# High-part products first for weight tiles whose low part is added by a transfer, and such low parts for one step of the down projection

## The chip, the cores and the metric

The kernel runs on one core of a Trainium2 chip. Its time is the device time of one execution, in microseconds; several executions give a median. The profile shows one execution of the same program with the start and end of every instruction. Engines are named as in the profile: PE (matrix products), PEld (loading of the stationary operand), ACT, DVE, POOL, and SP, which only issues transfers here; POOL issues transfers too.

## The reference

One decoder layer over 512 tokens of width 1024, in float32:

```python
u = rmsnorm(h, norm1_g)
proj = u @ w_in            # conv GLU | q | k | v | gate r | low-rank decay | merge gates
c = a_glu[..., :1024] * sigmoid(a_glu[..., 1024:])
c = silu(layernorm(causal_dwconv(c, width=31)));  y_conv = c @ w_conv_out
o = gla_chunked(q, k, v, decay);  y_gla = (rms(o) * silu(r)) @ w_gla_out
h = h + (sigmoid(gate_a) * y_conv + sigmoid(gate_b) * y_gla) @ w_o
z = causal_dwconv(rmsnorm(h, norm2_g) @ w_ffn_up, width=3)
h = h + (silu(z[..., :2816]) * z[..., 2816:]) @ w_ffn_down
return rmsnorm(h, final_g)
```

Every large product is made to nearly float32 precision from float32r parts: each operand is split into a high part and a low part (`x = hi + lo`), and three products are summed: low·high, high·low, high·high.

## The kernel before

**Tiles of weights.** All weights pass through one list, `order`, as tiles of 128 partitions by 1024 float32 (512 KB). `load()` issues the transfer of a tile into one of four `raw` buffers from SP. `split_weight()` makes the two parts in one of four `whi` and one of four `wlo` buffers: ACT copies `raw` to `hi`, which rounds it, and the low part is made in one of two ways. For most tiles DVE subtracts, `lo = raw - hi` (lines 324 and 351). For the tiles named in `ADDED` (part of `w_glu`, all of `w_qk`, `w_gb`, `w_gla`, part of `w_up`) ACT writes `lo = -raw` rounded in the same way (line 344), and POOL issues a transfer that reads the weight from DRAM a second time and adds it to `lo` (line 345). `weight()` hands a tile to the products and asks `prefetch(2)` to emit the splits of the next two tiles.

**Products.** `mm3` emits the three products of one block of 128 rows, lines 395, 396 and 397, in the order low·high, high·low, high·high of its two arguments. `col_tile` calls it eight times with the weights as the stationary operand: 24 products of 512 columns. The first needs `wlo`. This is used for `w_glu`, `w_qk`, the gates and the up projection.

**The down projection** (`seven`, also used for `w_o`) is a seven-product scheme over halves. Its 22 row tiles come in three groups of pairs (4, 3 and 4 pairs), each run after the up projection of the same rows. The steps of a group are listed in `STEPS`: `a11` for both halves d = 0 and 1 of its pairs, then `a12` d = 0, `s1` d = 0, `a12` d = 1, `s1` d = 1, and then `n2`, `s4`, `n3`, `a22`. Here the activations are the stationary operand and the weights move. Steps `a12` and `n3` use tiles as they are loaded; `a11`, `s1`, `n2` and `a22` work on tiles `kept` over several steps, into which sums are added by DVE (line 277) or by adding transfers from POOL (line 303, after the split of an earlier step). For `n3` a second block is added to the loaded one by a transfer from POOL (line 270, `add_n3`), which is issued when the load is.

**What sets the order.** Outside the stretches marked with `manual_schedule` (the start and the very end of the program), a framework orders each engine's instructions by its own estimate of times, and places the waits. Each engine then works through its own list in that order. A tile's buffer is handed on when its last reader is done.

**Other names below.** Line 813 is a tap of the causal convolution of width 31 on DVE, of which 240 are spread between other work. Line 1150 applies the gate to a head's output on DVE after a power taken on POOL (line 443), and line 1156 transposes that on PE. In the down projection the result of step `a12` is summed in PSUM tiles named `ax`, the others in tiles named `mm`; the activations of step `a12` are `ah` and `al`.

Of the kernel before, what the change touches and what calls it, by code (L numbers as in the profile page):

```python
# [10 lines left out]
F32 = mybir.dt.float32  # L11
# [3 lines left out]
AF = mybir.ActivationFunctionType  # L15
ALU = mybir.AluOpType

P = 128
D = 1024
T = 512  # L20
NT = T // P
KT = D // P
# [23 lines left out]
UP_SEVEN = (6, 7, 10, 11, 14, 15, 18)  # L46
UP_BESIDE = (1, 3, 4, 5, 9, 20, 13, 16, 17)
ADDED |= {("w_up", j) for i in UP_BESIDE for j in (i, FT + i)}
SEVEN = {"w_o": KT // 2, "w_down": FT // 2, "w_r": KT // 2, "w_v": KT // 2}


# [27 lines left out]
def trunk_layer(ctx: ExitStack, tc: tile.TileContext, a: dict, out: bass.AP):  # L79
    nc = tc.nc  # L80
# [88 lines left out]
    late = GLU_AT[0] + GLU_AT[1]  # L169
# [135 lines left out]
    def split_weight(between=None):  # L305
        if len(ready) < len(order):
            while len(raws) <= len(ready):
                load()
            raw = raws[len(ready)]
            name, spec = order[len(ready)]  # L310
            if name in SEVEN or name == "w_up7":
                raw = operand(name, raw, *spec) if name in SEVEN else up_operand(raw, *spec)
                n = raw.shape[-1]
                if name == "w_up7" and spec[1] == "m":
                    both = wp.tile([P, D], F32R, tag="raw", name=nm("wm"), bufs=4)
                    nc.scalar.copy(both[:, :T], raw)
                    nc.vector.tensor_tensor(both[:, T:], raw, both[:, :T].bitcast(F32), ALU.subtract)
                    ready.append((both[:, :T], both[:, T:]))
                    load()
                    return  # L320
                hi = wp.tile([P, D], F32R, tag="whi", name=nm("whi"), bufs=4)[:, :n]
                lo = wp.tile([P, D], F32R, tag="wlo", name=nm("wlo"), bufs=4)[:, :n]
                nc.scalar.copy(hi, raw)  # L323
                pace[0] = nc.vector.tensor_tensor(lo, raw, hi.bitcast(F32), ALU.subtract)  # L324
                if name in SEVEN:
                    sum_on(name, *spec)
                skipped = name in INNER and raws[len(ready)] is None
                ready.append((hi, lo))
                if not skipped:
                    load()  # L330
                return
            hi = wp.tile([P, D], F32R, tag="whi", name=nm("whi"), bufs=4)
            if order[len(ready)][0] == "w_low":
                nc.scalar.copy(hi, raw)
                if order[len(ready)][1] == 0:
                    part_lo = lambda t: t.rearrange("p (k c) -> p k c", c=P)[:, :, :RANK]
                    nc.vector.tensor_tensor(part_lo(hi), part_lo(raw), part_lo(hi.bitcast(F32)), ALU.subtract)
                ready.append((hi, None))
                load()
                return  # L340
            lo = wp.tile([P, D], F32R, tag="wlo", name=nm("wlo"), bufs=4)
            nc.scalar.copy(hi, raw)  # L342
            if order[len(ready)] in ADDED:
                pace[0] = nc.scalar.activation(lo, raw, AF.Copy, scale=-1.0)  # L344
                nc.gpsimd.dma_start(lo, a[name][spec], accum_op=ALU.add)  # L345
                ready.append((hi, lo))
                load()
                return
            if between:
                between()  # L350
            pace[0] = nc.vector.tensor_tensor(lo, raw, hi.bitcast(F32), ALU.subtract)  # L351
            ready.append((hi, lo))
            load()
# [37 lines left out]
    def mm3(acc, l, r, first, last, more=False):  # L391
# [4 lines left out]
        nc.tensor.matmul(acc, lh, rl, start=False, stop=False, **kw)  # L396
        nc.tensor.matmul(acc, lh, rh, start=False, stop=last, **kw)  # L397

    def col_tile(w, acts, acc=None, lo=0, hi=T):

        if acc is None:
            acc = mm_bank()
        for k in range(KT):
            s = slice(k * P, (k + 1) * P)
            ah, al = acts[k]
            mm3(acc[:, lo:hi], (w[0][:, s], w[1][:, s]), (ah[:, lo:hi], al[:, lo:hi]), k == 0, k == KT - 1)
        return acc

    def row_half(name, j0, n, acts, nk, done, tok_inner, middle=None):
# [856 lines left out]
    def seven(name, pairs, acts, complete, at=lambda step, i: None, fine=False):  # L1266
# [19 lines left out]
        def products(step, i, parts, lo=0, hi=T, own=None):  # L1286
            acc = bank[of[step]][i][:, lo:hi] if own is None else own[:, lo:hi]
            opens = step in ("a11", "s1", "a12") or own is not None
            for d, w in parts:
                for j, pair in enumerate(acts[2 * d : 2 * d + 2]):  # L1290
                    ah, al = (x[:, i * P : (i + 1) * P] for x in pair[step])
                    c = slice(j * T + lo, j * T + hi)

                    read = 2 * d + j == len(acts) - 1
                    mm3(acc, (ah, al), (w[0][:, c], w[1][:, c]), opens and d == 0 and j == 0, read, not opens)

        def add_to(t, n, c, x, op=ALU.add):
            nc.vector.tensor_tensor(hres[t, n][:, c], hres[t, n][:, c], x[:, c], op)  # L1298
# [287 lines left out]
    def by_parts(w):  # L1586

        acc = mm_bank()
        for k in range(KT):
            s = slice(k * P, (k + 1) * P)  # L1590
            mm3(acc, (w[0][:, s], w[1][:, s]), acts2[k], k == 0, k == KT - 1)
            yield acc

    for gi, pairs in enumerate(GROUPS):
        acts = []
# [123 lines left out]
```

## Time and profile before

| | us |
|---|---|
| median of 3 runs | 829.84 |
| lowest, highest | 829.54, 833.35 |
| the profiled execution | 828.47 |
| its span, first to last instruction | 826.8 |

The profiled execution took 828.47 us, of which 826.8 us are its span; about 1.7 us lie around it. A row of the timeline has the start in microseconds from the beginning of the span, the duration, engine and line, operation, what is written and what is read, and in brackets how long the engine sat idle before it and what ended that. A list of waits has engine and line, what it waited for, and then total microseconds, times, and the longest.

### The profile page before, as it was taken

The page shows a single profiled execution, that of the slowest core. Times are in us where ns is not written, and L with a number is a line of the kernel's source. Part 1 is how long each engine was busy: PE and PEld are TensorE (multiplying, and loading weights), DVE is VectorE, ACT ScalarE, POOL GpSimd, SP SyncE. Part 2 cuts the span into 40 slices and gives each one's busy share as a digit, 9 for nine tenths or more (in the row PEclk, how much of TensorE's full clock was granted, in tenths as well). Part 3 has the DMA queues.
Part 4 walks back from the last instruction along what each step waited for, and adds up shares of the span by engine and source line. Part 5 has one row for each costly group of instructions (what it writes and reads, how often), then busy time and mean ns, then how long its engine had stood idle before and what let it go on. Part 6 is the DMA issues. An engine that isn't in the chain of part 4 may idle for free.

```text
span 826.8 us, 11023 instructions
## 1 busy us (share of the span) xinstructions
PE 813.3 (98%) x4090; PEld 689.9 (83%) x4090; DVE 676.8 (82%) x991; ACT 471.0 (57%) x669; POOL 123.1 (15%) x144
## 2 busy tenths in 40 slices
PE   8999999999999999999999999999999999999996
PEld 7988878878888888888888898888788888988885
DVE  6898978999989889854689768789858888588896
ACT  7664546695443553359344659655446543667554
POOL 2021101311122121000001012111112111220111
PEclk9999999999999999999999999999999999999999
DMA  9999849558666578221447539356835647557562
GB/s 324 310 327 222 209 116 230 129 160 211 150 131 154 134 195 202 77 102 51 153 92 205 183 116 237 93 146 153 217 93 149 166 89 217 153 153 202 131 128 101
DMA packets 50213, 136.65 MB, mean 165 GB/s; under 512 B 4624, under 2 KB 17184, under 8 KB 50160
## 3 DMA queue, kind: packets, MB, share of 16 engines
q1 hardware_dynamic: 37456, 90.91, 31.2%
q0 software_dynamic: 12528, 44.83, 30.5%
q8 instruction: 32, 0.52, 0.3%
q10 hardware_dynamic: 176, 0.20, 0.1%
q14 instruction: 21, 0.17, 0.1%
HBM read 133.84 MB, written 6.29 MB: 169 GB/s over the span
## 4 chain that ended last, share of the span: by engine, by line
PE 78%; DVE 11%; DMA 4%; issue 3%; ACT 2%; POOL 1%; SPq 0%; POOLq 0%; ACTq 0%; DVEq 0%
PE mm L396 22%; PE mm L395 22%; PE mm L397 22%; DVE c L813 4%; PE ax L395 2%; DMA wlo<-in_w_glu_dram 2%; PE mm L663 2%; PE ax L396 2%; PE ax L397 2%; DVE wlo L324 1%; DMA kept<-rows 1%; DMA x<-in_x_dram 1%; PE ax L1137 1%; DVE tmp L1378 1%; PE ax L474 0%
## 5 line engine op out<-in xcount | busy, mean ns | idle before, releaser
L395 PE MATMUL mm<-uh,wlo 128*128 128x512 f32 (+1 forms) x636 | 237.5, 374 | 3.5 <-DMA wlo<-in_w_glu_dram 1.9
L396 PE MATMUL mm<-ul,whi 128*128 128x512 f32 (+1 forms) x636 | 234.9, 369 | 0.2 <-DVE ul L486 0.2
L397 PE MATMUL mm<-uh,whi 128*128 128x512 f32 (+1 forms) x636 | 234.5, 369 | 0.0
L813 DVE SCALAR_TENSOR_TENSOR c<-h,pp,c 128x507 f32<-128x507 f32 (+20 forms) x240 | 169.9, 733 | 2.8
L395 PEld LDWEIGHTS mm<-uh,wlo 128*128 128x128 f32 x636 | 119.9, 189 | 22.9 <-DMA wlo<-in_w_glu_dram 2.1
L397 PEld LDWEIGHTS mm<-uh,whi 128*128 128x128 f32 x636 | 119.8, 188 | 20.5
L396 PEld LDWEIGHTS mm<-ul,whi 128*128 128x128 f32 x636 | 120.1, 189 | 18.7 <-DVE ul L486 0.7
L342 ACT CAST whi<-raw 128x1024 fp32r<-128x1024 f32 x94 | 97.4, 1042 | 36.7 <-PE mm L397 29.0
L344 ACT ACTIVATE wlo<-raw 128x1024 fp32r<-128x1024 f32 x47 | 49.5, 1058 | 69.6 <-PE mm L395 65.5
L323 ACT CAST whi<-raw 128x1024 fp32r<-128x1024 f32 (+1 forms) x53 | 54.0, 1027 | 52.6 <-PE mm L397 36.1
L324 DVE TENSOR_TENSOR wlo<-raw,whi 128x1024 fp32r<-128x1024 f32 (+1 forms) x53 | 65.8, 1249 | 11.5 <-ACT whi L323 11.0
L1378 DVE SCALAR_TENSOR_TENSOR tmp<-mm,pp,tmp 128x511 f32<-128x511 f32 (+1 forms) x88 | 64.5, 742 | 12.6 <-ACT tmp L1376 12.2
L351 DVE TENSOR_TENSOR wlo<-raw,whi 128x1024 fp32r<-128x1024 f32 x47 | 56.9, 1220 | 16.7 <-ACT whi L342 16.3
L323 ACT CAST whi<-kept 128x1024 fp32r<-128x1024 f32 (+1 forms) x44 | 44.3, 1009 | 37.7 <-PE mm L397 25.6
L324 DVE TENSOR_TENSOR wlo<-kept,whi 128x1024 fp32r<-128x1024 f32 (+1 forms) x44 | 52.3, 1196 | 4.3 <-ACT whi L323 4.1
L1376 ACT ACTIVATE tmp<-mm,pp 128x512 f32<-128x512 f32 x44 | 33.3, 775 | 11.6 <-PE mm L397 11.6
L1298 DVE TENSOR_TENSOR hres<-hres,mm 128x512 f32<-128x512 f32 (+1 forms) x49 | 32.4, 670 | 2.5 <-PE mm L397 2.3
L345 POOL DMA_DIRECT2D wlo<-in_w_up_dram x18 | 15.6, 866 | 95.5 <-ACT wlo L344 77.6
L396 PE MATMUL mm<-wlo,sh 128*128 128x512 f32 x66 | 25.9, 393 | 0.0
L397 PE MATMUL mm<-whi,sh 128*128 128x512 f32 x66 | 25.7, 390 | 0.0
L395 PE MATMUL mm<-h,wlo 128*128 128x512 f32 x64 | 25.4, 397 | 0.0
L395 PE MATMUL mm<-whi,sl 128*128 128x512 f32 x66 | 25.2, 391 | 0.2 <-ACT whi L323 0.2
(361 smaller groups left out, 1635.1 us busy)
## 6 DMA issues: line engine op xcount, KB each, us to landing
raw<-in_w_up_dram SPq DMA_DIRECT2D x44, 512.0 KB, 4.4
wlo<-in_w_up_dram POOLq DMA_DIRECT2D x18, 512.0 KB, 7.4
raw<-in_w_glu_dram SPq DMA_DIRECT2D x16, 512.0 KB, 5.9
raw<-in_w_down_dram SPq DMA_DIRECT2D x15, 512.0 KB, 5.1
kept<-in_w_down_dram POOLq DMA_DIRECT2D x10, 512.0 KB, 5.3
raw<-in_w_v_dram SPq DMA_DIRECT2D x8, 512.0 KB, 6.0
rows<-in_w_r_dram SPq DMA_DIRECT2D x16, 256.0 KB, 6.4
raw<-in_w_qk_dram SPq DMA_DIRECT2D x8, 512.0 KB, 5.1
```

Of the source, the lines that this page charges most:

```text
L323: nc.scalar.copy(hi, raw)
L324: pace[0] = nc.vector.tensor_tensor(lo, raw, hi.bitcast(F32), ALU.subtract)
L342: nc.scalar.copy(hi, raw)
L344: pace[0] = nc.scalar.activation(lo, raw, AF.Copy, scale=-1.0)
L351: pace[0] = nc.vector.tensor_tensor(lo, raw, hi.bitcast(F32), ALU.subtract)
L395: nc.tensor.matmul(acc, ll, rh, start=first, stop=False, **kw)
L396: nc.tensor.matmul(acc, lh, rl, start=False, stop=False, **kw)
L397: nc.tensor.matmul(acc, lh, rh, start=False, stop=last, **kw)
L813: nc.vector.scalar_tensor_tensor(y[:, s:], c[:, : T - s], w, y[:, s:], ALU.mult, ALU.add)
L1298: nc.vector.tensor_tensor(hres[t, n][:, c], hres[t, n][:, c], x[:, c], op)
L1376: nc.scalar.activation(z, acc, AF.Identity, bias=pp[:, PP_FB + m : PP_FB + m + 1], scale=w[2])
L1378: nc.vector.scalar_tensor_tensor(z[:, s:], acc[:, : T - s], w[j], z[:, s:], ALU.mult, ALU.add)
```

## The change

It has three parts.

1. `col_tile` and `by_parts` now take their products from a new generator, `col_products`. For the tiles in a new set, `LOW_LAST_IN` (`w_glu` 4 and 8 and all eight of `w_qk`, all of them tiles whose low part is added), it emits the 16 products with `whi` first and the 8 with `wlo` behind them. For all other tiles the order is as before.
2. In the down projection the tiles of step `a12` (two per group, six in all, one of them half as wide) get their low part as the `ADDED` tiles do: ACT writes `-raw`, and POOL issues a transfer that adds the weight. The subtraction on DVE is gone for them.
3. In `products` of `seven`, the products of step `a12` are sorted so that within one half d the four with `whi` come before the two with `wlo` (two before one where a half has one pair). This holds for `w_o` too, whose low parts are still made by DVE.

```diff
+LOW_LAST_IN = {("w_glu", 4), ("w_glu", 8)} | {("w_qk", m) for m in range(KT)}
...
                 nc.scalar.copy(hi, raw)
-                pace[0] = nc.vector.tensor_tensor(lo, raw, hi.bitcast(F32), ALU.subtract)
+                if name == "w_down" and spec[1] == "a12":
+                    pace[0] = nc.scalar.activation(lo, raw, AF.Copy, scale=-1.0)
+                    src = block(name, spec[0], spec[2], *LOADS[spec[1]])
+                    nc.gpsimd.dma_start(lo, src, accum_op=ALU.add)
+                else:
+                    pace[0] = nc.vector.tensor_tensor(lo, raw, hi.bitcast(F32), ALU.subtract)
...
-                ready.append((hi, lo))
+                ready.append((hi, lo, (name, spec) in LOW_LAST_IN))
...
+    def col_products(w, acts, acc, lo=0, hi=T):
+        late = [(1, 0, k) for k in range(KT)] if w[2:] and w[2] else []
+        todo = [p for k in range(KT) for p in ([(0, 0, k), (0, 1, k)] if late else [(1, 0, k), (0, 1, k), (0, 0, k)])]
+        todo += late
+        for n, (low_w, low_a, k) in enumerate(todo):
+            l, r = w[low_w][:, k * P : (k + 1) * P], acts[k][low_a][:, lo:hi]
+            nc.tensor.matmul(acc[:, lo:hi], l, r, start=n == 0, stop=n == len(todo) - 1)
+            yield n
...
+            todo = []
             for d, w in parts:
                 for j, pair in enumerate(acts[2 * d : 2 * d + 2]):
...
+                    a = [x[:, i * P : (i + 1) * P] for x in pair[step]]
+                    b = [x[:, j * T + lo : j * T + hi] for x in w]
+                    todo += [(n, d, a[low_a], b[low_w]) for n, (low_a, low_w) in enumerate(((1, 0), (0, 1), (0, 0)))]
+                if step == "a12":
+                    todo.sort(key=lambda p: (p[1], p[0] == 1))
+            end = parts[-1][0] == (len(acts) - 1) // 2
+            kw = {} if opens else {"skip_group_check": True}
+            for n, (_, d, l, r) in enumerate(todo):
+                nc.tensor.matmul(acc, l, r, start=opens and d == 0 and n == 0, stop=end and n == len(todo) - 1, **kw)
```

How this moves instructions is shown for three places. A row has the line, the operation, what is written, what is read, and the shape; the lines of the changed kernel are later by the lines added.

The first is PE at the tile `w_glu` 8 (`whi_1068`, `wlo_1069`; `uh` and `ul` are the activations). Before, its start:

```order
L397 MATMUL mm_981<-whi_1032,f_814 128x512
L395 MATMUL mm_1121<-uh_105,wlo_1069 128x512
L396 MATMUL mm_1121<-ul_106,whi_1068 128x512
L397 MATMUL mm_1121<-uh_105,whi_1068 128x512
L395 MATMUL mm_1121<-uh_105,wlo_1069 128x512
```

With the change, its start and its end:

```order
L403 MATMUL mm_981<-whi_1032,f_814 128x512
L412 MATMUL mm_1121<-uh_105,whi_1068 128x512
L412 MATMUL mm_1121<-ul_106,whi_1068 128x512
...
L412 MATMUL mm_1121<-ul_108,whi_1068 128x512
L412 MATMUL mm_1121<-uh_105,wlo_1069 128x512 x4
L412 MATMUL mm_1121<-uh_107,wlo_1069 128x512 x4
L401 MATMUL mm_979<-whi_1075,ul_108 128x512
```

The low part was read by the first product of the tile and is now read by the last eight, behind sixteen others.

The second is POOL's list of transfers in the first group of the down projection (`kept` are sums for `s1` and `a22`, `raw` are the second blocks of `n3`, `wlo_5069` and `wlo_5149` the low parts of `a12` d = 0 and 1). Before:

```order
L303 DMA kept_4851<-in_w_down_dram 128x1024
L303 DMA kept_4874<-in_w_down_dram 128x1024
L270 DMA raw_5185<-in_w_down_dram 128x1024
L270 DMA raw_5208<-in_w_down_dram 128x1024
L303 DMA kept_4851<-in_w_down_dram 128x1024
```

With the change:

```order
L304 DMA kept_4851<-in_w_down_dram 128x1024
L304 DMA kept_4874<-in_w_down_dram 128x1024
L328 DMA wlo_5069<-in_w_down_dram 128x1024
L271 DMA raw_5187<-in_w_down_dram 128x1024
L328 DMA wlo_5149<-in_w_down_dram 128x1024
L271 DMA raw_5210<-in_w_down_dram 128x1024
L304 DMA kept_4851<-in_w_down_dram 128x1024
```

Two transfers are added, and the second stands behind one that adds to the tile of `n3` d = 0. In the other two groups the order is the same.

The third is ACT at the same place (`tmp` is the convolution of the up projection's last tiles). Before:

```order
L323 COPY whi_5068<-raw_4932 128x1024
L1376 ACTIVATE tmp_5058<-mm_4949,pp 128x512
L323 COPY whi_5086<-kept_4851 128x1024
L1376 ACTIVATE tmp_5093<-mm_4924,pp 128x512
L1376 ACTIVATE tmp_5098<-mm_4925,pp 128x512
L323 COPY whi_5147<-raw_4990 128x1024
```

With the change:

```order
L326 ACTIVATE wlo_5069<-raw_4932 128x1024
L324 COPY whi_5068<-raw_4932 128x1024
L1394 ACTIVATE tmp_5058<-mm_4949,pp 128x512
L324 COPY whi_5087<-kept_4851 128x1024
L1394 ACTIVATE tmp_5094<-mm_4924,pp 128x512
L1394 ACTIVATE tmp_5099<-mm_4925,pp 128x512
L326 ACTIVATE wlo_5149<-raw_4990 128x1024
L1409 COPY yh_5064<-w_5052 128x512
L324 COPY whi_5148<-raw_4990 128x1024
```

ACT writes the negative of each `a12` tile ahead of its high part, and one instruction of another kind comes between them for d = 1.

More of the change, by code (lines that the diff above doesn't have):

```diff
@@ L402, in col_tile @@
             acc = mm_bank()
[L403 to L406, printed above, removed]
+        for _ in col_products(w, acts, acc, lo, hi):
+            pass
         return acc
@@ L1288, in products @@
             opens = step in ("a11", "s1", "a12") or own is not None
+            todo = []
             for d, w in parts:
                 for j, pair in enumerate(acts[2 * d : 2 * d + 2]):
[L1291 to L1295, printed above, removed]
+                    a = [x[:, i * P : (i + 1) * P] for x in pair[step]]
[7 more added lines that the diff above has]
+                nc.tensor.matmul(acc, l, r, start=opens and d == 0 and n == 0, stop=end and n == len(todo) - 1, **kw)
         def add_to(t, n, c, x, op=ALU.add):
@@ L1588, in by_parts @@
         acc = mm_bank()
[L1589 to L1592, printed above, removed]
+        for n in col_products(w, acts2, acc):
+            if n % 3 == 2:
+                yield acc
     for gi, pairs in enumerate(GROUPS):
```

## The prediction

> **What bounds the kernel now.** First the page: which engine is full, and at what clock.
>
> ```profile
> span 826.8 us, 11023 instructions
> PE 813.3 (98%) x4090; PEld 689.9 (83%) x4090; DVE 676.8 (82%) x991; ACT 471.0 (57%) x669; POOL 123.1 (15%) x144
> PEclk9999999999999999999999999999999999999999
> ```
>
> PE is busy for 98% of the span, and the granted clock is full in every slice. A change that leaves the number of products alone, as this one does, can only take PE's waits away or add some. So the second view is the list of what PE waited for.
>
> ```profile
> PE mm L395 <- DMA wlo<-in_w_glu_dram: 1.9, 2, 1.7
> PE mm L395 <- DMA wlo<-in_w_qk_dram: 1.6, 1, 1.6
> PE ax L1156 <- DVE o L1150: 0.2, 1, 0.2
> PE mm L395 <- ACT whi L323: 0.2, 1, 0.2
> ```
>
> Waits for an added low part come to 3.5 us, all in `w_glu` and `w_qk`, none in the down projection, where DVE makes the low parts. That is all there is to win, with 0.2 us where `whi` is late. The timeline places them.
>
> ```profile
> 60.90 0.47 PE L395 MATMUL mm<-uh,wlo 128*128 128x512 f32 x1 [0.19 <-DMA wlo<-in_w_glu_dram]
> 106.38 0.50 PE L395 MATMUL mm<-uh,wlo 128*128 128x512 f32 x1 [1.69 <-DMA wlo<-in_w_glu_dram]
> 106.72 0.39 PE L396 MATMUL mm<-ul,whi 128*128 128x512 f32 x1
> 183.56 0.50 PE L395 MATMUL mm<-uh,wlo 128*128 128x512 f32 x1 [1.60 <-DMA wlo<-in_w_qk_dram]
> ```
>
> **Part 1, high products first in `w_glu` and `w_qk`.** Undisturbed, one product starts 0.227 us after the last (the rows at 569.12 and 569.34 below). Sixteen products ahead of the first low one give 16 x 0.227 = 3.6 us of cover, more than the longest of these waits, 1.7 us. So the waits at 60.90 and 106.38 go: 0.19 + 1.69, and the product after a wait also runs 0.1 us longer (0.50 against 0.39), twice: 2.1 us. Is that kept? Behind them comes a stretch in which DVE is full:
>
> ```profile
> 127.57 1.22 DVE L324 TENSOR_TENSOR wlo<-raw,whi 128x1024 fp32r<-128x1024 f32 x1 [1.74 <-ACT whi L323]
> 126.49 1.05 ACT L323 CAST whi<-raw 128x1024 fp32r<-128x1024 f32 x1 [1.91 <-PE mm L933]
> 137.00:212.00 75.00, 73.40 (x335) 60.91 (x334) 72.17 (x113) 53.80 (x77) 14.61 (x15) 1.00 0.69 175
> 212.11 0.88 DVE L1150 SCALAR_TENSOR_TENSOR o<-ax,rstd,h 128x256 f32<-128x256 f32 x2 [0.60 <-POOL rstd L443]
> 212.66 0.83 PE L1156 MATMUL ax<-ident,o 128*128 128x128 f32 x3 [0.17 <-DVE o L1150]
> ```
>
> The third row is a window; its fourth figure is DVE: 72.2 of 75 us busy. At its end PE waits for DVE (212.66). Up to 127.57 DVE still waits for ACT, and ACT for PE, so an earlier PE makes DVE earlier, and the 2.1 us pass. The wait at 183.56 lies inside the stretch: without it PE reaches 212.66 by 1.7 us sooner and stands there for the same DVE result. I count it at nothing. Bounds of part 1: 1.9 gained (the waits alone) and 3.8 (if DVE gave way to the third as well).
>
> **Parts 2 and 3, the down projection.** Removed from DVE: five subtractions of 1.22 us and one half as wide. DVE is not what PE waits for here, but for 0.2 us of `whi` and the stretched product after it in the first group, which follow sums that DVE makes late; I count 0.3 us gained. Added to ACT: six writes of about 1.06 us, on an engine that is idle for 43%. What matters is when the low part is ready. In the first group:
>
> ```profile
> 562.39 1.05 ACT L323 CAST whi<-raw 128x1024 fp32r<-128x1024 f32 x1 [1.76 <-PE mm L397]
> 561.65 0.86 POOL L303 DMA_DIRECT2D kept<-in_w_down_dram  x1 [1.22 <-DVE wlo L324]
> 569.12 0.39 PE L395 MATMUL ax<-whi,al 128*128 128x512 f32 x1
> 569.34 0.39 PE L396 MATMUL ax<-wlo,ah 128*128 128x512 f32 x1
> 568.68 1.05 ACT L323 CAST whi<-raw 128x1024 fp32r<-128x1024 f32 x1 [1.43 <-issue]
> 572.33 0.87 POOL L270 DMA_DIRECT2D raw<-in_w_down_dram  x1 [9.81 <-PE mm L397]
> 575.94 0.39 PE L395 MATMUL ax<-whi,al 128*128 128x512 f32 x1
> 560.00:570.00 10.00, 10.00 (x57) 8.76 (x57) 8.59 (x13) 5.92 (x8) 1.29 (x2) 1.00 0.83 209
> ```
>
> The last row is a window again: the last figure but one, 0.83, is the share of the transfer engines. The buffers of `a12` d = 0 come free at 562.39. ACT now writes the negative first, to 563.45, and POOL issues the adding transfer about 0.4 us later, 563.9. How long it takes has to come from others:
>
> ```profile
> wlo<-in_w_up_dram POOLq DMA_DIRECT2D x18, 512.0 KB, 7.4
> wlo<-in_w_glu_dram POOLq DMA_DIRECT2D x5, 512.0 KB, 10.8
> kept<-in_w_down_dram POOLq DMA_DIRECT2D x10, 512.0 KB, 5.3
> raw<-in_w_down_dram SPq DMA_DIRECT2D x15, 512.0 KB, 5.1
> ```
>
> The last figure is the median from issue to landing: 5.3 us for adding transfers with room, 7.4 for `w_up`, 10.8 where several queue up. Here the window 560 to 570 already has the transfer engines at 0.83, with two `kept` transfers ahead and loads from SP alongside. I take 8.7, nearer the middle of 7.4 and 10.8: landed at 572.6. Sorting puts four products ahead, so the low part is needed at 569.12 + 4 x 0.227 = 570.0. PE waits 2.6 us.
>
> The low part of d = 1 has a worse path. Its negative can be written at 568.7, but its transfer stands on POOL behind the one for `n3` (line 270), which before was issued at 572.33. That one waits for a load: the row names PE, but PE's products run on without break and the load, one of three from SP, is the last thing it needs:
>
> ```profile
> 565.20 0.50 SPq L258 DMA_DIRECT2D raw<-in_w_down_dram  x1
> DMA to landing us min/median/max: 6.4/6.4/6.4
> ```
>
> 565.20 + 6.4 = 571.6. So the low part is issued at 572.33 + 0.87 = 573.2 at best; with the first added transfer competing with that load I put it 1.5 us later, 574.7 (an estimate: half of the 3 us or so by which the medians above spread). With the 7.2 us that the `n3` transfer itself took in the same place, it lands at 581.9. It is needed at 575.94 + 0.91 = 576.85. So PE is held 5.1 us by then, and the 2.6 us of d = 0 are part of it, since they make d = 1 late as well. Bounds: issue at 573.2 and 5.3 us gives 1.6; issue at 574.7 and 10.8 gives 8.7. I take 5.1, near the middle of these.
>
> Groups two and three have more room:
>
> ```profile
> 663.55 1.04 ACT L323 CAST whi<-raw 128x1024 fp32r<-128x1024 f32 x1
> 671.91 0.39 PE L395 MATMUL ax<-whi,al 128*128 128x512 f32 x1
> 670.29 0.88 POOL L270 DMA_DIRECT2D raw<-in_w_down_dram  x1 [8.57 <-DVE tmp L1378]
> 677.36 0.39 PE L395 MATMUL ax<-whi,al 128*128 128x512 f32 x1
> 784.40 0.87 POOL L270 DMA_DIRECT2D raw<-in_w_down_dram  x1 [7.40 <-DVE tmp L1378]
> 786.06 1.06 ACT L323 CAST whi<-raw 128x1024 fp32r<-128x1024 f32 x1 [2.36 <-PE mm L397]
> 792.66 0.39 PE L395 MATMUL ax<-whi,al 128*128 128x512 f32 x1
> ```
>
> Group two, d = 0: about 1.5 us after 663.55 to the issue, 5.3 to land, 670.4, against a need at 672.8: hidden. Its d = 1 is half a tile: issued at some 671.9 behind line 270, with 5.3 for a whole one it lands at 677.2 at the latest when alone; needed at 677.8. I add 0.4 us for a small slip (bounds 0 and 1.5). Group three, d = 1: issued 1.5 us after the buffer's release near 785.7, 787.2, behind line 270 of 784.40; landing after 5.3 to 7.4 us is 792.5 to 794.6, needed at 793.6. I add 0.8 (bounds 0 and 4.4, at 10.8 us).
>
> **The sum.** -2.1 - 0.3 + 5.1 + 0.4 + 0.8 = +3.9 us. The profiled execution took 828.47 (826.8 span, 1.7 around it), which gives 832.4; the median of the runs is 1.4 us higher, 829.84, which gives 833.7. I forecast halfway, 833.0. About 0.5%, 4.1 us, is what a measurement of this kernel can tell from no change, so this is slower by an amount at that edge.
>
> **Rivals.** *The added low parts hide* (not slower). The mechanism is a short transfer: if those in the first group land in 5.3 us with the `n3` load unhindered, only 1.6 us of the wait at d = 1 is left, groups two and three wait for nothing, and the sum is -2.1 - 0.3 + 1.6 = -0.8: 828.4 on the same base of 829.2. It decides from a landing below 6.5 us on. For it: half of the ten issues in the row of `kept`, at 5.3 and less. Against it: the 0.83 of the window. The Trainium skill, page "DMA: Bandwidth & Descriptors", section "Anatomy of one DMA", fits a transfer from POOL as 2.0 us plus the bytes by 436 GB/s, 3.2 us for a tile as an estimate; by that even d = 1 is in before 576.85 and the sum is -2.4. The rows speak against it for adding transfers, whose medians are 5.3 and up.
>
> *The third wait counts too* (faster): the rival above and the 1.7 us at 183.56 kept, as if DVE's taps (line 813) made room: -2.5, 826.7. The 0.17 us at 212.66 speaks against it.
>
> *Adding transfers pile up in every group* (slower by more): each `a12` transfer takes the 10.8 us of the queued ones. Then group one waits 8.7, group two 1.5, group three 4.4, and the sum is -2.4 + 14.6 = +12.2: 841.4. It decides where three adding transfers are in flight at once, which the new order on POOL makes possible in the first group alone.
>
> *PE starts slow after a long wait.* At its very start twelve small products take 2.93 us, and eight of the same size 1.09 a little later:
>
> ```profile
> 1.12 2.93 PE L532 MATMUL ax<-ones 128*128 128x128 f32 x12 [1.12 <-DVE ones L499]
> 4.61 1.09 PE L474 MATMUL ax<-ident,x 128*128 128x128 f32 x8 [0.36 <-DMA x<-in_x_dram]
> ```
>
> If a wait brings that state back, the half of 2.9 us, 1.5, is lost after each; with two in the first group +3.0 more, 836.1. The Trainium skill, page "TensorE: Matmul & The Clock Gate", section "HAM oscillation", has the clock halved after idle gaps over some 3.4 us; my two waits of 2.6 and 2.5 us stay below. No wait of this trace is long enough to show it.
>
> **How the numbers follow.** Forecast 55%, hidden 22%, third wait 4%, pile-up 13%, slow start 6%. Around the forecast its own terms reach from +1 to +7, 830 to 836. Range: below, half of the hidden case, 827.5; above, slow start and the mild half of the pile-up, 838. Slower by over 0.5% (833.99 on the median): nearly half of the forecast (0.24), pile-up and slow start: 0.42. Faster by over 0.5% (825.7) needs the third case and luck: 0.05. The rest is 0.53.
>
> **What would show it.** In the changed profile PE should have no wait for `wlo<-in_w_glu_dram` or `w_qk`; the wait at L1156 on PE near 211 should grow by about 1.7 us. New waits of PE for `wlo<-in_w_down_dram` should total 5 to 7 us, most of it before 585 and in two pieces, and the transfer for d = 1 there should be issued right behind that of line 271, after 573. I am wrong if these waits total under 2 us, if the one for d = 1 ends by its ACT write rather than by line 271's place in POOL's list, or if PE gains at 183 without losing at 212.

## The result, and the profile after

| | before | changed |
|---|---|---|
| median of the runs, us | 830.62 (829.54 to 833.35, 4 runs) | 840.44 (838.88 to 841.91, 4 runs) |
| the profiled execution, us | 828.47 | 839.51 |
| its span, us | 826.8 | 837.8 |

The ratio is 1.0113, with a 95% interval from 1.0082 to 1.0145: slower by 1.1%, some 9.8 us, where 833.0 was forecast and 838 was the upper end of the range. The two profiled executions differ by 11.04 us.

The page of the changed kernel shows PE as full as before, with 4.2 us more of busy time for the same 4090 products:

```profile
span 837.8 us, 11048 instructions
PE 817.5 (98%) x4090; PEld 692.7 (83%) x4090; DVE 671.2 (80%) x985; ACT 477.0 (57%) x675; POOL 128.4 (15%) x150
```

Its list of what PE waited for:

```profile
PE ax L1313 <- DMA wlo<-in_w_down_dram: 8.0, 4, 2.6
PE ax L1169 <- DVE o L1163: 1.5, 1, 1.5
PE ax L401 <- ACT mm L1584: 1.2, 1, 1.2
```

No wait for `w_glu` or `w_qk` is left. There are four new ones for low parts of the down projection (line 1313 is now the product in `products`), one for the gated output where PE transposes it (lines 1163 and 1169, before 1150 and 1156), and one at 552. PE's timeline at these places:

```profile
210.91 1.16 PE L1169 MATMUL ax<-ident,o 128*128 128x128 f32 x6 [1.48 <-DVE o L1163]
...
552.45 0.39 PE L401 MATMUL ax<-n,wlo 128*128 128x256 f32 x1 [1.24 <-ACT mm L1584]
...
569.37 0.39 PE L1313 MATMUL ax<-whi,ah 128*128 128x512 f32 x1
572.13 1.12 PE L1313 MATMUL ax<-wlo,ah 128*128 128x512 f32 x2 [2.37 <-DMA wlo<-in_w_down_dram]
573.04 0.63 PE L1313 MATMUL ax<-whi,al 128*128 128x512 f32 x1
573.47 0.63 PE L1313 MATMUL ax<-whi,ah 128*128 128x512 f32 x1
...
575.88 0.39 PE L1313 MATMUL mm<-whi,yl 128*128 128x512 f32 x1
...
580.45 0.39 PE L1313 MATMUL ax<-whi,ah 128*128 128x512 f32 x1
582.93 0.73 PE L1313 MATMUL ax<-wlo,ah 128*128 128x512 f32 x2 [2.09 <-DMA wlo<-in_w_down_dram]
...
683.09 0.39 PE L1313 MATMUL ax<-whi,ah 128*128 128x512 f32 x1
684.40 0.50 PE L1313 MATMUL ax<-wlo,ah 128*128 128x512 f32 x1 [0.92 <-DMA wlo<-in_w_down_dram]
...
799.84 0.39 PE L1313 MATMUL ax<-whi,ah 128*128 128x512 f32 x1
802.86 0.73 PE L1313 MATMUL ax<-wlo,ah 128*128 128x512 f32 x2 [2.64 <-DMA wlo<-in_w_down_dram]
...
804.36 1.03 PE L1313 MATMUL ax<-wlo,ah 128*128 128x512 f32 x2
...
808.00 0.39 PE L1313 MATMUL mm<-wlo,sh 128*128 128x512 f32 x1
```

A product that waits for nothing starts 0.227 us after the last. From 569.37 to 572.13 are 2.76 us, so 2.53 are lost; at 582.93 it is 2.25, at 684.40 1.08, at 802.86 2.79: 8.65 us together. Behind two of the four something else follows. After 572.13 the products start 0.43 us apart (573.04, 573.47), until 575.88: nine of them take 3.75 us instead of 2.04. Between 804.36 and 808.00 again nine take 3.64. That is 1.71 + 1.60 = 3.3 us. The windows view shows why (behind the busy times the granted clock, the share of the transfer engines, GB/s):

```profile
573.00:575.00 2.00, 2.00 (x6) 1.56 (x5) 0.07 (x1) 0.01 (x1) 0.94 (x2) 0.50 0.10 41
583.00:585.00 2.00, 2.00 (x9) 1.65 (x10) 0.69 (x1) 0.00 (x0) 0.86 (x1) 1.00 0.70 115
805.00:807.00 2.00, 2.00 (x6) 1.54 (x6) 1.71 (x4) 1.21 (x3) 1.35 (x2) 0.50 0.89 129
```

The clock is halved after the gaps at 572.13 and 802.86 and full after the one at 582.93. PE counts as busy there, which is where most of the 4.2 us come from.

POOL's rows show how the low parts came so late (in order: a sum for `s1`, the low part for d = 0, the addition for `n3` d = 0, the low part for d = 1; then the last three in the third group):

```profile
561.22 0.86 POOL L304 DMA_DIRECT2D kept<-in_w_down_dram  x1 [1.23 <-DVE wlo L330]
563.18 0.87 POOL L328 DMA_DIRECT2D wlo<-in_w_down_dram  x1 [1.10 <-ACT wlo L326]
574.06 0.85 POOL L271 DMA_DIRECT2D raw<-in_w_down_dram  x1 [10.01 <-DMA raw<-in_w_down_dram]
574.69 1.10 POOL L328 DMA_DIRECT2D wlo<-in_w_down_dram  x1
...
784.05 0.87 POOL L328 DMA_DIRECT2D wlo<-in_w_down_dram  x1 [0.55 <-ACT wlo L326]
792.87 0.85 POOL L271 DMA_DIRECT2D raw<-in_w_down_dram  x1 [7.95 <-DMA raw<-in_w_down_dram]
793.79 0.86 POOL L328 DMA_DIRECT2D wlo<-in_w_down_dram  x1
```

The times from issue to landing of those at 561.22, 563.18, 574.06, 574.69, 792.87 and 793.79, one line for each:

```profile
DMA to landing us min/median/max: 7.0/7.0/7.0
DMA to landing us min/median/max: 8.9/8.9/8.9
DMA to landing us min/median/max: 5.2/5.2/5.2
DMA to landing us min/median/max: 8.2/8.2/8.2
DMA to landing us min/median/max: 5.2/5.2/5.2
DMA to landing us min/median/max: 9.0/9.0/9.0
```

Add issue and duration: 568.2 and 572.1; 579.3 and 582.9; 798.1 and 802.8. Each of these three low parts lands 3.6 to 4.7 us behind the adding transfer ahead of it in POOL's list, though it was issued only 0.6 to 2.0 us behind it.

Where the 11 us are, against the terms of the forecast:

| | forecast | profile of the change |
|---|---|---|
| waits for `w_glu` and `w_qk` gone, part lost at 211 | -2.1 | -1.75 |
| lost again at 552 | 0 | +1.3 |
| `whi` no longer late in the first group | -0.3 | -0.4 |
| first group, waits for low parts (4.8) and half clock between the two (1.7) | +5.1 | +6.5 |
| second group | +0.4 | +1.1 |
| third group, waits for low parts | +0.8 | +2.8 |
| third group, half clock behind the wait | 0 | +1.6 |
| sum | +3.9 | +11.1 |

The start of the n-th product of the two executions differs by -1.75 us behind 211, -0.44 behind 552.45 and +11.03 at the end.

### The profile page after: what moved, and what is told of

Same layout as the page of the kernel before. It is cut to its first block, busy times and chain, and to the rows that moved or that the text cites. A ratio compares the mean times of both kernels' runs of the same rounds, so it can differ in the third digit from the quotient of the medians.

```text
span 837.8 us, 11048 instructions
## 1 busy us (share of the span) xinstructions
PE 817.5 (98%) x4090; PEld 692.7 (83%) x4090; DVE 671.2 (80%) x985; ACT 477.0 (57%) x675; POOL 128.4 (15%) x150
## 4 chain that ended last, share of the span: by engine, by line
PE 79%; DVE 11%; DMA 5%; ACT 3%; issue 1%; POOL 0%; SPq 0%; POOLq 0%; ACTq 0%; DVEq 0%
PE mm L412 48%; PE mm L1313 11%; DVE c L826 4%; DMA wlo<-in_w_down_dram 3%; PE mm L403 2%; PE mm L402 2%; PE mm L401 2%; PE mm L676 2%; PE ax L401 1%; PE ax L402 1%; PE ax L403 1%; PE ax L1313 1%; DVE wlo L330 1%; DMA raw<-in_w_down_dram 1%; DMA x<-in_x_dram 1%
## 5 line engine op out<-in xcount | busy, mean ns | idle before, releaser
L412 PE MATMUL mm<-ul,whi 128*128 128x512 f32 (+1 forms) x608 | 227.1, 374 | 0.2 <-DVE ul L499 0.2
L412 PE MATMUL mm<-uh,whi 128*128 128x512 f32 (+1 forms) x608 | 226.5, 373 | 0.0
L412 PE MATMUL mm<-uh,wlo 128*128 128x512 f32 (+1 forms) x608 | 217.1, 377 | 0.0
L412 PEld LDWEIGHTS mm<-uh,whi 128*128 128x128 f32 x608 | 114.5, 188 | 20.4
L412 PEld LDWEIGHTS mm<-uh,wlo 128*128 128x128 f32 x608 | 114.5, 189 | 18.7 <-DMA wlo<-in_w_glu_dram 0.6
L412 PEld LDWEIGHTS mm<-ul,whi 128*128 128x128 f32 x608 | 114.7, 189 | 18.4 <-DVE ul L499 0.7
L1396 DVE SCALAR_TENSOR_TENSOR tmp<-mm,pp,tmp 128x511 f32<-128x511 f32 (+1 forms) x88 | 64.6, 743 | 14.6 <-ACT tmp L1394 14.1
L330 DVE TENSOR_TENSOR wlo<-raw,whi 128x1024 fp32r<-128x1024 f32 (+1 forms) x47 | 59.0, 1264 | 12.2 <-ACT whi L324 11.7
L412 PE MATMUL mm<-h,whi 128*128 128x512 f32 x128 | 39.5, 389 | 0.0
L412 PEld LDWEIGHTS mm<-h,whi 128*128 128x128 f32 x128 | 24.0, 188 | 5.2 <-issue 0.2
```

The costliest lines, as they stand in the source:

```text
L412: nc.tensor.matmul(acc[:, lo:hi], l, r, start=n == 0, stop=n == len(todo) - 1)
L1396: nc.vector.scalar_tensor_tensor(z[:, s:], acc[:, : T - s], w[j], z[:, s:], ALU.mult, ALU.add)
```

## The experiments

All ratios are to the kernel before on the same chip, in the same rounds. Its median there was 833.56 for *cols_only*, *cols_glu_only*, *cols_fewer_taps* and *down_only*, 831.64 for *n3_behind*, *unsorted*, *half0_only* and *late_groups*, 832.18 for *change_again*, *cols_again*, *cols_ten_taps* and *sorted_no_add*, and 832.41 for *no_waits* and *glu_three*; its single executions lay between 828.4 and 838.1 us, so the profiled one, 828.47, is among its shortest. "Part 1 alone" is the changed kernel with these two edits:

```diff
-                if name == "w_down" and spec[1] == "a12":
+                if False:
...
-                if step == "a12":
+                if False:
```

**Part 1 alone, and its halves.** *cols_only* is part 1 alone.

> Part 1 alone: high products first in w_glu and w_qk, the down projection as before. Theory A (DVE is full up to line 1150, and a load of the up projection at 541 sets a second limit): PE is 3.5 us ahead behind the w_qk tile at 183, 1.75 us ahead behind the transpose of line 1150's result at 211, and between 0.4 and 1.75 us ahead at the end, so about 829 to 830 beside 830.6 for the kernel before. Rival B (the third wait counts in full): 3.5 us ahead to the end, 827. Rival C (sorting the products costs PE something the profile does not list): not ahead at all.

829.23 us, ratio 0.9943 [0.9923, 0.9963]. On a third chip it ran again as *cols_again*:

> Part 1 alone, once more. Theory A from the profiles: 0.4 to 1.75 us faster than the kernel before, a ratio of 0.998 to 0.9995; the 0.9943 of the other chip is the same kernel. Rival K (part 1 also does away with waits that the profile of the kernel before does not show, since these transfers land later in other executions than in the profiled one): a ratio of 0.995 or less again.

829.65 us, ratio 0.9975 [0.996, 0.9989]. So rival C falls, and the gain is 2.5 to 4.3 us, more than the 1.75 by which PE is ahead behind 211 in the profile of the change. Neither theory has both runs: 0.9943 meets K's bound and not A's range, and 0.9975 lies between the two. *cols_glu_only* takes `w_qk` out:

```diff
-LOW_LAST_IN = {("w_glu", 4), ("w_glu", 8)} | {("w_qk", m) for m in range(KT)}
+LOW_LAST_IN = {("w_glu", 4), ("w_glu", 8)}
```

> Part 1 for the two w_glu tiles alone; w_qk and the down projection as before. Theory A: PE waits again for the low part of w_qk near 182 (1.6 us), but reaches the transpose of line 1150's result 1.75 us ahead all the same, with a wait there under 0.5 us, so the time is within 0.3 us of part 1 for all tiles. Rival B: w_qk is worth 1.75 us of its own, so this kernel is that much slower than part 1 for all tiles.

828.06 us, ratio 0.9934 [0.9911, 0.9956], the same as with `w_qk` within the intervals. Its waits:

```profile
PE mm L412 <- DMA wlo<-in_w_qk_dram: 1.2, 2, 1.0
...
PE ax L1169 <- DVE o L1163: 0.2, 1, 0.2
```

PE waits for `w_qk` and then hardly for line 1163. With part 1 for all tiles it is the other way round, and worse than even: behind the 1.47 us at 211 the clock is halved in that execution. *cols_again*:

```profile
211.03 1.72 PE L1169 MATMUL ax<-ident,o 128*128 128x128 f32 x6 [1.47 <-DVE o L1163]
...
213.40 0.63 PE L412 MATMUL mm<-uh,whi 128*128 128x512 f32 x1
```

So the third wait is worth nothing, as A had it. *glu_three* adds `w_glu` 6 to the two tiles, again without `w_qk`:

> Part 1 for w_glu 4, 6 and 8, without w_qk; the down projection as before. In four profiles with part 1 the low part of w_glu 6 is waited for near 72, 0.5 to 1.8 us, which the profile of the kernel before does not show. Theory A with rival K (low parts of w_glu land later in some executions than in the profiled one, and part 1 covers that): no wait for w_glu near 72, and 0.5 to 1.5 us less than part 1 without w_glu 6 had: a ratio of 0.992 to 0.996. Otherwise (DVE sets the time behind that tile): the ratio of part 1 for w_glu 4 and 8 or above, 0.994 to 0.998.

827.99 us, ratio 0.9951 [0.9932, 0.997]. The wait near 72 is gone from its list, but the interval covers the ratios of both outcomes: no decision.

**Why PE waits at 211.** *cols_fewer_taps* is part 1 alone with `"w_qk": 4.0` instead of 4.5 in `RATES`, the taps of the convolution per weight tile.

> Part 1 alone, and four convolution taps (3 us of DVE) moved from the w_qk tiles to later tiles. Theory A: with DVE no longer full up to 212, the wait of PE for line 1150 falls from 1.5 us to under 0.5 us and PE is about 3.2 us ahead at 211, where part 1 alone gives 1.75. Rival D (the wait at line 1150 comes from a chain through POOL's power, line 443, and not from DVE's load): the wait stays at 1.5 us and nothing is gained.

829.49 us, ratio 0.9952 [0.9934, 0.9971]; PE's wait stayed at 1.5 us. The trial says nothing, since 122 of the 240 taps stand ahead of the first line 1163 on DVE in both kernels: the rate moved none past it. *cols_ten_taps* has `"w_v": 0.5` instead of 1, which moves ten.

> Part 1 alone, with ten convolution taps (7.3 us of DVE) taken from the stretch ahead of the first line 1150 and put behind it; the earlier trial with four taps moved none of them past that line. Theory A (the wait there follows DVE's load, through ACT's squares that stand behind a row that waits for DVE): the wait of PE falls from 1.5 us to under 0.5 us, and PE is 1.2 to 1.7 us further ahead there than with part 1 alone. Rival D (it follows from the power on POOL between two results of line 1150): it stays at 1.5 us.

833.02 us, ratio 1.0 [0.9983, 1.0018], slower than part 1 alone. PE's wait of 1.46 us stayed, so theory A's prediction fails; PE also waits 1.3 us for another result of DVE (line 833), which it does not with part 1 alone. But D is not shown either: the stretch in which taps were taken away is 160 to 185, and in the last 24 us ahead of the result DVE is busy for 23.9 us all the same (23.1 with part 1 alone):

```profile
160.00:185.00 25.00, 19.53 (x32) 1.00 0.64 156
185.00:209.00 24.00, 23.89 (x47) 1.00 0.91 217
```

**Parts 2 and 3 alone.** *down_only*:

```diff
-LOW_LAST_IN = {("w_glu", 4), ("w_glu", 8)} | {("w_qk", m) for m in range(KT)}
+LOW_LAST_IN = set()
```

> Parts 2 and 3 alone: the products of w_glu and w_qk in their old order. Theory A: the down projection loses the same 11 us by itself (four waits for added low parts, 8.7 us in all, and two stretches at half the granted clock, 3.5 us in all, against 0.4 us gained by the earlier high part), so 841 to 842.5. Rival E (the earlier PE of part 1 is what makes the low parts late): the waits shrink by what part 1 had gained at 552, 0.4 us in each, and with them one of the half-clock stretches, so about 838.

842.53 us, ratio 1.0116 [1.0086, 1.0147]. By the medians that is 9.0 us above the kernel before on its chip, between A's 11 and E's 7.4, so the time does not decide. The profile does: the waits for low parts did not shrink (9.6 us idle, against 8.0 in the changed kernel), so E's mechanism falls. There is one half-clock stretch, in the third group; the one in the first group is missing. One gap longer than that at 572.13 in the changed kernel was not followed by one:

```profile
583.55 0.72 PE L1313 MATMUL ax<-wlo,ah 128*128 128x512 f32 x2 [3.14 <-DMA wlo<-in_w_down_dram]
```

**Sorting without adding.** *change_again* and *sorted_no_add* ran beside *cols_again*. The first is the changed kernel, the second the changed kernel with only the first of the two edits above (parts 1 and 3).

> The changed kernel once more, on the chip on which part 1 alone, part 3 without added low parts and the variant with ten taps moved run. Theory A (parts 2 and 3 cost the 11 us that the first profile of the change shows behind 552): 11 us slower than part 1 alone. Rival J (part 1 alone was measured on a chip on which the kernel before was slow by chance, 833.6 where it was 830.6 elsewhere): part 1 alone is within 0.2% of the kernel before here, and the change 9.5 to 10 us above both.

839.62 us, ratio 1.0088 [1.007, 1.0106], 10.0 us above part 1 alone on the same chip, near A's 11. Part 1 alone is 0.25% below the kernel before there, nearer to J's 0.2% than to the 0.57% of the first chip; but the change is 7.4 us above the kernel before, and not the 9.5 to 10 us of J.

> Parts 1 and 3 without part 2: the products of a12 are sorted, but DVE still subtracts for their low parts. Theory A: no wait for a low part in the down projection and the time of part 1 alone within 0.15%: all of the 11 us comes with the added transfers. Rival L (sorting itself, which lets the last low part's products end the tile, holds buffers longer): 1 us or more slower than part 1 alone.

828.84 us, ratio 0.9964 [0.9946, 0.9982]. No wait for a low part of `w_down`. L falls; this run and *change_again* differ by part 2 alone, so the 10 us come with the added transfers.

**What the sorting saves.** *unsorted* is the changed kernel with the second of the two edits above.

> The changed kernel without part 3: the products of a12 in the old order, so that the second product of a tile needs the low part. Theory A: each of the four waits is 0.7 us longer (three products of 0.227 us less cover), and in the first group d = 1 passes 2.4 us of idle PE and gets a half-clock stretch of its own of 1.5 to 1.9 us: 3 + 1.7 = 4.7 us slower than the changed kernel, 845. Rival H (the half clock depends on the pattern of products and not on the length of the gap): 3 us slower, 843.5, with two stretches as before.

841.25 us, ratio 1.0117 [1.0097, 1.0136], beside 1.0113 and 1.0088 for the change: both expectations are too high. Three products of cover are worth 0.3 us by the one ratio and 2.4 us by the other; the runs do not settle which. The profile has four waits again:

```profile
PE ax L1313 <- DMA wlo<-in_w_down_dram: 8.7, 4, 3.3
```

Three are longer by 0.4 to 0.6 us. The one for d = 1 in the first group is shorter (1.23 us idle): there the transfer lands at 583.1, within 0.3 us of where it did, and PE comes later by what it lost at d = 0.

**Which tiles.** *half0_only* and *late_groups* restrict the added low parts:

```diff
-                if name == "w_down" and spec[1] == "a12":
+                if name == "w_down" and spec[1] == "a12" and spec[2] == 0:
...
-                if name == "w_down" and spec[1] == "a12":
+                if name == "w_down" and spec[1] == "a12" and spec[0] != GROUPS[0]:
```

> The changed kernel with the low part of a12 added by a transfer for d = 0 alone; d = 1 is subtracted by DVE again. Theory A: only the first group waits for a low part, 2.5 us with a half-clock stretch of 1.9 us behind it; the other groups wait for none: 830.6 - 0.4 - 0.4 + 4.4 = about 834. Rival I (the transfers for d = 0 alone take the room of later loads in every group): over 836.

831.14 us, ratio 0.9994 [0.9979, 1.0009]. One wait, 2.4 us, with a half-clock stretch, as A has it. A's 834 is 3.4 us above the kernel before; measured are 0.5 us below it. Of the 3.9 us between, the larger gain of part 1 (2.5 us on another chip, where A put in 0.4) would explain 2.1; the rest stays open. Rival I falls.

> The changed kernel with added low parts for a12 in the second and third group alone; the first has DVE subtract. Theory A: waits of 1.1 us in the second and 2.8 us in the third group, and there a half-clock stretch of 1.6 us: 830.6 - 0.4 + 5.5 = about 835.5. Rival E2 (the second and third group are late only because the first one is): waits under 1 us in all and no stretch, about 830.5.

835.57 us, ratio 1.0042 [1.0026, 1.0058]. Two waits, 3.0 us idle, so E2 falls. No half-clock stretch behind them in the profiled execution, where A had one.

**POOL's list.** *n3_behind* puts one transfer behind another:

```diff
+            if name == "w_down" and d == 0:
+                with tc.issue_after(added[0].ins):
+                    add_n3(name, pairs, d)
-            if name not in INNER:
+            elif name not in INNER:
...
-                    nc.gpsimd.dma_start(lo, src, accum_op=ALU.add)
+                    added[0] = nc.gpsimd.dma_start(lo, src, accum_op=ALU.add)
```

> The changed kernel, with the transfer that adds n3's second block (d = 0) put behind the added low part of a12 d = 1 in POOL's list, in all three groups. Theory A (POOL's list and the sharing of the transfer engines with that transfer make d = 1 late): the low part of a12 d = 1 is issued near 569 in the first group instead of 574.7 and lands before its need, in the other two groups it takes under 6 us from issue to landing instead of 6.6 and 9.0; three of the four waits go (2.25, 1.08 and 2.8 us) and the half-clock stretch of the third group (1.6 us), so about 833 beside 840.4; the wait for d = 0 in the first group, 2.5 us, and its half-clock stretch stay. Rival F (the transfer engines are full in these stretches whatever the order): the low parts land within 1 us of where they did, 839 to 841. Rival G: the n3 transfer becomes the late one, a wait for it at step n3 of 1 us or more.

830.84 us, ratio 0.999 [0.9976, 1.0005]: 1.0 to 1.2% below the change. PE's waits for low parts and POOL's rows (line 332 is the low part, 275 the addition for `n3`):

```profile
PE ax L1317 <- DMA wlo<-in_w_down_dram: 1.7, 1, 1.7
```

```profile
569.89 0.85 POOL L332 DMA_DIRECT2D wlo<-in_w_down_dram  x1 [5.39 <-ACT wlo L330]
574.18 0.86 POOL L275 DMA_DIRECT2D raw<-in_w_down_dram  x1 [3.44 <-DMA raw<-in_w_down_dram]
...
788.37 0.84 POOL L332 DMA_DIRECT2D wlo<-in_w_down_dram  x1 [8.88 <-ACT wlo L330]
789.00 1.10 POOL L275 DMA_DIRECT2D raw<-in_w_down_dram  x1
```

The landings of the last two:

```profile
DMA to landing us min/median/max: 5.3/5.3/5.3
DMA to landing us min/median/max: 9.3/9.3/9.3
```

The two have changed places: the low part now takes 5.3 us and the addition behind it 9.3, which nobody waits for. Three waits and the stretch in the third group are gone, and PE waits for no `n3` tile; F and G fall. The fourth wait is shorter than A had it, 1.7 us of idle time, and has no half clock behind it, which is one reason why the time is below A's 833.

**All waits taken away.** *no_waits* is *n3_behind* with DVE's subtraction for the one low part that was still late, d = 0 of the first group:

```diff
-                if name == "w_down" and spec[1] == "a12":
+                if name == "w_down" and spec[1] == "a12" and not (spec[0] == GROUPS[0] and spec[2] == 0):
```

> The changed kernel with n3's added block (d = 0) behind the added low part of a12 d = 1 in POOL's list, and with DVE subtracting for a12 d = 0 of the first group alone; five of the six low parts stay added by transfers. Theory A (the loss is the four waits and the half-clock stretches behind them): no wait for a low part of w_down over 0.3 us, and the time of part 1 alone, a ratio of 0.994 to 0.998 to the kernel before. Rival M (added transfers in the down projection cost something besides the waits, by the load of the transfer engines on later tiles): 1.000 or more.

828.99 us, ratio 0.9955 [0.9939, 0.9971]. No wait for a low part of `w_down` is in its list, and the time is that of part 1 alone. Five added low parts cost nothing by themselves that these runs can tell; M falls. This version beats both kernels, as does part 1 alone, which is simpler.

## Why the prediction was wrong

Two steps failed. In the third group "landing after 5.3 to 7.4 us is 792.5 to 794.6" gave 0.8 us of wait, where 2.8 were lost. And half clock behind a wait was put at nothing, because "my two waits of 2.6 and 2.5 us stay below" the length from which it was expected; gaps of 2.37 and 2.64 us were followed by it, and in the third group it cost 1.6 us. The terms in turn:

- **The waits at 60.90 and 106.38 go, and the third is worth nothing** (-2.1): right. PE was 3.6 us ahead behind 183 and 1.75 behind 211, and without `w_qk` the time is the same within the intervals. That DVE's load is the reason was only argued; the trial with ten taps did not bear it out, and it stays open. In the timed runs part 1 gains 2.5 to 4.3 us. The one profile of the kernel before is among its fastest executions, so differences from it understate a gain; how much of the rest that explains stays open too.
- **Kept to the end**: not in the profiled execution, which lost 1.3 us at 552. Ahead of it on DVE a sum (line 286) waits 5.83 us for a load of `w_up`, until 540.78, and PE goes on at 552.45, 11.67 us later. In all 16 profiles these two are 11.65 to 11.68 us apart, in the kernel before too (541.21 and 552.89), so this sum sets PE there, and in 12 of them the profile ends the sum's wait with the load. The load is issued 1.73 us earlier in the changed kernel, as PE is ahead, but the sum starts 5.80 us behind that issue, where the kernel before has 4.50; the other profiles have 4.8 to 6.3. The two profiles of the changed kernel have 5.80 and 4.82 us there, so 1.0 of the 1.3 us belongs to the execution and not to the change. The one profile of the kernel before has the shortest time of all; whether the last 0.3 us is its luck is not shown.
- **The first group** (+5.1): right in place and cause, and short by 1.4 us. The low part of d = 1 was issued right behind line 271 at 574.69, where 574.7 stood in the prediction, but took 8.2 us and not 7.2, and PE came there 0.4 us earlier. The 4.8 us of waits alone look like the forecast only because 1.7 us of half clock lie between them. That stretch costs nothing of its own: PE is held until d = 1 lands. *change_again* has a stretch there and *down_only* has none, and against the kernel before both lose 5.2 us between 567 and 590.
- **The third group** (+0.8, measured 2.8): mis-sized. The step that failed is "landing after 5.3 to 7.4 us is 792.5 to 794.6". It counted from the low part's own issue and took the addition for `n3` to be 2.8 us ahead, as before. But the load that this addition waits for now runs beside the first added low part: it is issued at 785.79 and holds POOL's next row until 792.87 (the rows above), 7.08 us, where the kernel before has 3.88 from its issue to the addition. The eight profiles without added low parts have 3.8 to 4.3 us there, the six with one ahead and the old order of POOL's list 7.0 to 8.2. So the addition went out 0.92 us ahead of the low part, which landed 4.7 us behind it, 9.0 us after its issue. The same chain had been put into the first group and left out here.

```profile
785.79 0.33 SPq L259 DMA_DIRECT2D raw<-in_w_down_dram  x1
```

- **The second group** (+0.4, measured 1.1): within its bounds, for the same reason.
- **"PE starts slow after a long wait"** was a rival with 6%, set aside because the waits would stay below the gap that the prediction cites for it. Its price per stretch was near (1.5 forecast, 1.6 and 1.7 measured), and so was the forecast gap (2.6 us, measured 2.4 idle); the point from which it decides was not. Its place was not either: it had both stretches in the first group, where one costs nothing of its own, and the 1.6 us that count are in the third.

The third group is the largest miss: 2.0 us of wait and 1.6 of half clock more than forecast. With 1.4 in the first group, 0.7 in the second, 1.3 at 552 and about 0.3 less from part 1, the forecast of 3.9 becomes the 11 us; the median of the change then lies 2.4 us above the range. The rival of piled-up transfers came near in time (841.4) by luck and by other means: it had 14.6 us of waits and no half clock. In the rival of hidden low parts, the estimated transfer that has d = 1 in before 576.85 has it so only from an issue at 573.2; from the forecast's own 574.7 it ends at 577.9. Of the signs that the prediction named, the total of the waits was missed, 8.0 us idle against 5 to 7. The chance of "slower" was 0.42, below that of "same".

## What to carry to other kernels

In these runs, adding transfers of one queue that overlap land one behind the other. A full-size low part landed 3.6 to 4.7 us behind the adding transfer ahead of it in the rows above, and 2.5 to 5.1 us in the other profiles but for one case of 6.1; a forecast from its own issue and a median came out too early. So first write down what stands ahead of it in that list and what that one waits for; changing the places of two transfers was worth 1.0 to 1.2% of the kernel. And where an engine is full at full clock, a wait of over 2 us is priced with what may follow it, here 1.6 us more in 8 of 12 cases, unless a later wait would hold the engine anyway.

## What the runs showed of the hardware

**Half clock behind gaps.** In the profiles with waits for low parts of `w_down`, gaps of 2.1 to 3.5 us idle were followed by a stretch at half the granted clock in 8 of 12 cases, gaps under 1.8 us there in none. The stretches begin at once (572.13) or 1.5 us later (804.36), and a gap of 3.14 us had none, so the length of the gap alone does not decide. The traces' lists of clock states sort these cases. Each stretch lasts 3.41 us there, and the two of the changed kernel begin at 572.27 and 804.38, 68 times 3.413 us apart; the other profiles keep to such a grid as well. Counted in the windows of this grid, PE was idle for 1.9 to 2.9 us in the window just ahead of each of the eight stretches, and for at most 1.8 us in any window around the other four gaps. The first two rows are the windows ahead of the two stretches of the changed kernel, the others the three at the gap of 3.14 us in *down_only* (3.41 less the second figure is PE's idle time):

```profile
568.86:572.27 3.41, 1.04 (x5) 0.54 (x5) 3.41 (x5) 2.17 (x4) 0.00 (x0) 1.00 1.02 341
800.97:804.38 3.41, 1.52 (x7) 1.26 (x8) 0.75 (x2) 0.99 (x2) 0.64 (x2) 1.00 0.18 56
```

```profile
578.31:581.72 3.41, 2.10 (x10) 1.41 (x8) 3.41 (x5) 0.84 (x1) 0.00 (x0) 1.00 1.06 202
581.72:585.13 3.41, 1.58 (x7) 1.33 (x8) 1.11 (x2) 0.00 (x0) 0.86 (x1) 1.00 1.05 203
585.13:588.54 3.41, 3.41 (x17) 2.80 (x16) 2.53 (x4) 0.93 (x1) 0.00 (x0) 1.00 0.84 156
```

Idle are 2.37 and 1.89 us ahead of the stretches; the long gap is split into 1.31 and 1.83 us. Behind the 1.47 us at 211, where PE does small transposes on both sides, 8 of 12 profiles with that wait have a stretch: there 1.6 to 1.8 us idle in a window went with one, and at most 1.5 with none. This sorting was found in the traces afterwards, and no run tried it. The Trainium skill, page "TensorE: Matmul & The Clock Gate", gives 3.4 us as the gap to stay below (section "HAM oscillation") and a free-running window of that length (Part 1). The length of the stretches and their grid agree with such a window; the figure of 3.4 us as a safe length does not, since 2.37 us was enough at 572.13.

**The start.** The first products run at half speed for a time that differs between executions. In the window from 1 to 11 us PE starts 45 products in the profiled execution of the kernel before and 40 in that of *cols_glu_only*, whose order is the same there, while the granted clock is shown as 1.00 in both (the first row is the kernel before):

```profile
1.00:11.00 10.00, 8.61 (x45) 7.23 (x46) 5.86 (x10) 6.37 (x13) 2.13 (x10) 1.00 0.91 343
```

```profile
1.00:11.00 10.00, 9.44 (x40) 8.41 (x41) 5.06 (x9) 5.67 (x11) 2.13 (x10) 1.00 0.92 353
```

A pair of 128x512 products takes 0.73 us at 6.89 in the one and 1.20 us at 7.16 in the other. The traces' lists of clock states begin with the first full clock, at 4.13 us in the one and 10.22 us in the other, and the column shows 1.00 ahead of that too. Five products of 0.227 us are over 1 us between executions that do the same work in the same order.
